# Spare accumulation banks behind each group of eight columns, mixer steps on ScalarE, and the output transfers in another order

## The chip, the cores and the metric
The kernel runs on one core of a Trainium2 chip. The metric is the time of one execution on the device in microseconds (us). Three runs of the kernel before took 987.56 to 987.98 us, with a median of 987.88 us.

## The reference
Two blocks of a transformer follow each other on one sequence of 256 tokens with 1024 channels, all in float32.

```
x = x + rms_norm(hybrid_mixer(rms_norm(x)) @ w_out)          # block 1: RG-LRU, gated linear
h = rms_norm(x)                                              # attention (GLA), causal softmax attention
x = x + rms_norm((silu(h @ w_gate) * (h @ w_up)) @ w_down)   # FFN 0
for l in (0, 1):                                             # block 2, with shifts and scales from c
    h = modulate(x, sh1, sc1)
    y = short_conv_mixer(h) if l == 0 else forgetting_attention(h, k, v, log_fcum)
    x = layer_norm(alpha * x + g1 * y)
    h = modulate(x, sh2, sc2)
    x = layer_norm(alpha * x + g2 * swiglu(h))               # FFN 1 and FFN 2
```

The widths of the FFNs are 2816. The second attention has 16 heads of 64. The gated linear attention works with the logarithm of a forget gate, `log_sigmoid(...) / 16`, which is summed along chunks of 64 tokens and goes through exponentials. The shifts, scales and gates of block 2 are products of `silu(c)` with matrices of 112 x 128 rows.

## The kernel before
All activations lie transposed, 128 channels by 256 tokens to a tile, so that x is eight tiles. Weights are streamed in blocks of 128 x 128; there are 2336 of them. Eight blocks come with one transfer of 512 KB (`raw_load`, line 127), issued on SyncE's (SP's) queue, into one of four buffers. To reach float32 accuracy, each weight and each activation is held as a high and a low part. `weights` (line 130) splits eight blocks at a time: ScalarE (ACT) copies them into the high part `wh` (line 144), and VectorE (DVE) subtracts to get the low part `wl` (line 150). There are five buffers for each part. A block then costs three matmuls on TensorE (PE): high by high, low by high and high by low (`mm3`, lines 162 to 164).

The results go to eight accumulation banks (PSUM). Four belong to the pool `pacc` (tiles named acc), two to `plg` (named lg), and two to `pms` (named ms, for small things). `single` (line 168) computes one output column of 128 channels in one acc bank, `pair` (line 176) two columns in one acc bank. `kouter` (line 223) computes eight columns at once, with the loop over the eight input tiles outermost, so that it can begin before all tiles of the input are there; it takes all four acc banks. `lazy` (line 1041) begins six columns of an FFN or of the key projection before the normalisation of its input is known, four in acc and two in lg banks.

Each FFN (`ffn`, line 900) has 22 pairs of a gate column and an up column. FFN 0 begins with a group of eight columns in `kouter` and goes on with 18 pairs. FFN 1 and FFN 2 have six lazy columns, then a group of eight, then 15 pairs. After each pair `evac` (line 906) reads the bank: in FFN 0 DVE multiplies both columns by the row R (lines 909 and 911), ACT applies silu (line 522), DVE multiplies (line 914), ACT makes the high part (line 921) and DVE the low part `ml` (line 922). In FFN 1 and 2 the multiplications by R fall away and line 918 reads the bank. The down projection (22 blocks to a column) follows. The convolution stage (lines 1201 to 1223) has 24 columns: a group of eight, and then singles.

The matrices of the shifts and scales are handled by `gemv` (line 360): one transfer of 512 KB for 128 rows, on SP's queue, into one of three buffers gw (line 368), and one product on DVE with a sum along the row (line 371). 112 of them are spread over the work by `fill` (line 184): after each column `grate` of them come due (`GR`, line 30: 0.75 per column in FFN 0, 1.2 in its down projection, 0.375 in the convolution stage, 0.9 and 1.05 in FFN 1 and its down projection, 1.4 in the second attention, 0.25 in FFN 2; a column of a down projection counts 2.75). In the second attention only the query columns from number 3 on count, five of them.

The order on every engine is written by a scheduler that simulates the program at compile time with modelled durations; it puts what is ready in the simulation first, and by the order of the program among what is ready. `after` (line 383) ties one instruction behind another on the same engine. Two sets of ties matter here. `unbroken` (line 377) sets `bound`, a list of instructions behind which the coming splits `wl` are put (after `free` of them), and `gbound`, the instruction behind which the coming products of `gemv` are put. In FFN 0 `gbound` is the end of the reciprocal root before it.

The second attention (lines 1304 to 1322) is written with a fixed order on PE. In step i of its loop PE computes the query column of pair i + 1, the logits of pair i, the transposes of the softmax of pair i - 1 (`fox_pt`, line 800), four blocks of the output projection, and the product with the values. The softmax (`fox_softmax`, line 784) takes four maxima on DVE (line 793), four exponentials on ACT (line 794), one reciprocal and four normalisations on DVE (line 797). Before the loop, splits are tied behind the forget gates; behind step 0, splits and products are tied behind the last maximum of pair 0.

In the mixer, `lru` (line 529) takes four taps of a convolution on DVE, `gla_decay` (line 599) adds a bias and divides by 16 on DVE (lines 607 and 615), and `gla` (line 618) masks the keys for four heads on DVE (line 643). At the end six output tiles are finished on DVE (lines 1355 and 1357) and tiles 0 and 1 on GpSimd (POOL) and ACT; each tile's transfer is issued on SP's queue (line 1358).

## Time and profile before

| what | value |
|---|---|
| median of three runs | 987.88 us |
| the profiled execution, its own time | 985.9 us |
| its span, from the first to the last instruction | 984.2 us |
| mean granted clock of PE | 0.979 of full speed |
| bytes moved by transfers | 219.56 MB, 223 GB/s over the span |

The profiled execution is one run of the program. Its time is the span and 1.7 us around it. A row of the timeline has the start and the length in us from the span's start, the engine, the line of the kernel, the operation with its output and inputs, and the count; in brackets stands how long the engine was idle before it and what ended that. Consecutive instructions of the same kind are merged into one row. The busy time of PE counts matmuls that overlap, so a busy PE is not PE at its peak.

### The profile page before, as it was taken

What the parts mean: (1) busy time and instruction counts of PE and PEld (TensorE: products, weight loads), DVE (VectorE), ACT (ScalarE), POOL (GpSimd) and SP (SyncE); (2) the same over time, 40 slices, a digit from 0 to 9 for tenths busy, and PEclk for the clock granted to TensorE, in tenths of its full rate; (3) what the DMA queues carried; (4) which work ended last, traced back from release to release, by engine and by line L of the source; (5) the groups of instructions that cost most, each with busy time, mean ns of one, the idle gap of its engine ahead of it and who ended that gap; (6) DMA issues with size and microseconds to landing.
All of it is one profiled execution on the core that took longest, in us unless ns stands there. A gap on an engine that the chain in (4) does not pass through costs nothing.

```text
span 984.2 us, 19003 instructions
## 1 busy us (share of the span) xinstructions
PE 927.9 (94%) x7434; PEld 893.6 (91%) x7434; DVE 768.8 (78%) x1471; ACT 530.2 (54%) x951; POOL 19.7 (2%) x66
## 2 busy tenths in 40 slices
PE   7989997999999999998899999999699999999996
PEld 7879896999999899998899999987587899999995
DVE  7896678999988588679899899796764897665553
ACT  7484653554444555548555454377365586554331
POOL 1111000000000000000000000000000000000001
PEclk9999998999999999999999999999799999999998
DMA  8754337899999477544999999454642257655531
GB/s 291 249 197 129 108 108 278 294 330 327 318 336 390 142 255 250 179 134 155 320 341 356 329 368 348 167 176 145 250 150 65 87 153 275 214 184 183 191 108 43
DMA packets 62346, 219.56 MB, mean 223 GB/s; under 512 B 7112, under 2 KB 8784, under 8 KB 62256
## 3 DMA queue, kind: packets, MB, share of 16 engines
q1 hardware_dynamic: 61056, 215.06, 63.7%
q0 software_dynamic: 1056, 3.16, 1.0%
q8 instruction: 58, 0.95, 0.4%
q14 instruction: 32, 0.26, 0.1%
q10 hardware_dynamic: 144, 0.13, 0.0%
HBM read 217.26 MB, written 2.63 MB: 223 GB/s over the span
## 4 chain that ended last, share of the span: by engine, by line
PE 80%; DVE 12%; ACT 4%; issue 3%; DMA 2%; DVEq 0%; ACTq 0%
PE acc L162 20%; PE acc L164 20%; PE acc L163 20%; PE acc L197 4%; DVE wl L150 4%; PE acc L198 4%; PE acc L203 3%; DMA raw<-wts 1%; ACT wh L144 1%; DVE gw L371 1%; PE acc L251 1%; PE acc L253 1%; PE acc L252 1%; PE ms L820 1%; PE lg L773 1%
## 5 line engine op out<-in xcount | busy, mean ns | idle before, releaser
L150 DVE TENSOR_TENSOR wl<-raw,wh 128x1024 fp32r<-128x1024 f32 (+2 forms) x296 | 356.2, 1209 | 102.4 <-ACT wh L144 101.0
L144 ACT ACTIVATE wh<-raw 128x1024 fp32r<-128x1024 f32 (+2 forms) x296 | 307.6, 1046 | 225.4 <-PE acc L164 128.2
L162 PE MATMUL acc<-yh,wh 128*128 128x256 f32 x608 | 171.1, 282 | 7.0 <-DVE ff_m L918 5.6
L162 PE MATMUL acc<-xh,wh 128*128 128x256 f32 x576 | 164.2, 285 | 8.9 <-DVE ff_u L911 7.2
L164 PE MATMUL acc<-yl,wh 128*128 128x256 f32 x608 | 171.3, 282 | 0.0
L163 PE MATMUL acc<-yh,wl 128*128 128x256 f32 x608 | 170.6, 281 | 0.0
L163 PE MATMUL acc<-xh,wl 128*128 128x256 f32 x576 | 162.9, 283 | 1.4 <-DVE wl L150 1.4
L164 PE MATMUL acc<-xl,wh 128*128 128x256 f32 x576 | 163.0, 283 | 0.0
L163 PE MATMUL acc<-mh,wl 128*128 128x256 f32 x528 | 148.1, 281 | 0.0
L164 PE MATMUL acc<-ml,wh 128*128 128x256 f32 x528 | 148.1, 281 | 0.0
L162 PE MATMUL acc<-mh,wh 128*128 128x256 f32 x528 | 147.9, 281 | 0.0
L371 DVE SCALAR_TENSOR_TENSOR gw<-gw,cact 128x1024 f32<-128x1024 f32 x112 | 134.7, 1221 | 0.6 <-DMA gw<-ada 0.4
L162 PEld LDWEIGHTS acc<-yh,wh 128*128 128x128 f32 x608 | 115.2, 190 | 7.6 <-DVE ff_m L918 6.1
L162 PEld LDWEIGHTS acc<-xh,wh 128*128 128x128 f32 x576 | 109.9, 191 | 11.3 <-DVE ff_u L911 7.4
L163 PEld LDWEIGHTS acc<-yh,wl 128*128 128x128 f32 x608 | 115.2, 190 | 0.4 <-issue 0.4
L164 PEld LDWEIGHTS acc<-yl,wh 128*128 128x128 f32 x608 | 114.9, 189 | 0.6 <-issue 0.6
L163 PEld LDWEIGHTS acc<-xh,wl 128*128 128x128 f32 x576 | 110.1, 191 | 1.8 <-DVE wl L150 1.6
L164 PEld LDWEIGHTS acc<-xl,wh 128*128 128x128 f32 x576 | 109.8, 191 | 0.1
L162 PEld LDWEIGHTS acc<-mh,wh 128*128 128x128 f32 x528 | 99.5, 189 | 0.0
L164 PEld LDWEIGHTS acc<-ml,wh 128*128 128x128 f32 x528 | 99.4, 189 | 0.0
L163 PEld LDWEIGHTS acc<-mh,wl 128*128 128x128 f32 x528 | 99.3, 188 | 0.0
L197 PE MATMUL acc<-xh,wh 128*128 128x256 f32 (+1 forms) x256 | 67.7, 294 | 8.7 <-ACT wh L144 5.5
(399 smaller groups left out, 1493.2 us busy)
## 6 DMA issues: line engine op xcount, KB each, us to landing
raw<-wts SPq DMA_DIRECT2D x288, 512.0 KB, 4.5
gw<-ada SPq DMA_DIRECT2D x112, 512.0 KB, 5.6
raw<-wts SPq DMA_DIRECT2D x6, 256.0 KB, 5.9
m_scr<-m_row POOLq DMA_DIRECT2D x2, 768.0 KB, 5.8
ax<-xT SPq DMA_DIRECT2D x4, 256.0 KB, 4.8
m_b<-m_scr POOLq DMA_DIRECT2D x8, 128.0 KB, 3.6
out<-fg SPq DMA_DIRECT2D x8, 128.0 KB, 1.8
cst<-cst SPq DMA_DIRECT2D x1, 588.5 KB, 7.1
```

Of the source, the lines that this page charges most:

```text
L144: i = self.aw = nc.scalar.activation(self.wh[:, d], r, AF.Copy)
L150: self.anchor = nc.vector.tensor_tensor(self.wl[:, d], r, self.wh[:, d].bitcast(F32), ALU.subtract)
L162: m = [mm(ps, wh, xh, start=start, stop=False), mm(ps, wl, xh, start=False, stop=False), mm(ps, wh, xl, start=False, stop=stop)]
L163: mm(ps, wl, xh, start=False, stop=False),
L164: mm(ps, wh, xl, start=False, stop=stop)]
L197: m.append(mm(outs[i], wh, X[0][k], start=k == 0 and i % per == 0, stop=False))
L198: m.append(mm(outs[i], wl, X[0][k], start=False, stop=False))
L203: m.append(mm(outs[i], wh, X[1][k], start=False, stop=False))
L251: mm(outs[tt], h, wh, start=k == 0 and (tt == 0 or not one), stop=False)
L252: mm(outs[tt], l, wh, start=False, stop=False)
L253: mm(outs[tt], h, wl, start=False, stop=k == NK - 1 and (tt == 1 or not one))
L371: i = nc.vector.scalar_tensor_tensor(t, t, 1.0, self.cact, op0=ALU.mult, op1=ALU.mult, accum_out=self.ada[:, g:g + 1])
```

## The change
`single` and `pair` get a switch that puts their result into an lg bank. The two pairs behind each group of eight in an FFN, and the two singles behind it in the convolution stage, use it. In `ffn`, `gbound` becomes the last write of each evacuation. In the second attention, splits are tied behind the last normalisation of an earlier pair and products behind that of the pair just issued. In the mixer the first tap of the convolution (two instructions), the bias of the gate (one) and the head masks (four) go from DVE to ACT, and the division by 16 goes into the scale of the exponentials. The output transfers are issued behind the loop in a given order.

```diff
+OUT = (2, 3, 4, 5, 0, 6, 1, 7)
...
-    def single(self, wname, c, X, nk=NK, fill=True):
-        t = self.acc([P, T])
+    def single(self, wname, c, X, nk=NK, fill=True, spare=False):
+        t = self.tl(self.plg, [P, T], "lg") if spare else self.acc([P, T])
...
-    def pair(self, w0, c0, w1, c1, X):
-        t = self.acc([P, 2, T])
+    def pair(self, w0, c0, w1, c1, X, spare=False):
+        t = self.tl(self.plg, [P, 2, T], "lg") if spare else self.acc([P, 2, T])
...
-            V.tensor_scalar(xc, xpad[:, 0:T], self.vec("lru_conv_w", t), self.vec("lru_conv_b", t), ALU.mult, ALU.add)
+            A.activation(xc, xpad[:, 0:T], AF.Identity, scale=self.vec("lru_conv_w", t), bias=self.vec("lru_conv_b", t))
...
-        V.tensor_scalar(z[:, 0:T], zp, self.vec("gla_gate_b", 0), None, ALU.add)
+        self.nc.scalar.activation(z[:, 0:T], zp, AF.Identity, bias=self.vec("gla_gate_b", 0))
...
-        la = la[:, 0:T]
-        V.tensor_scalar(la, la, 1.0 / 16.0, None, ALU.mult)
-        return la
+        return la[:, 0:T]
...
-        A.activation(ex, cum, AF.Exp)
+        A.activation(ex, cum, AF.Exp, scale=1.0 / 16)
...
-        A.activation(en, cum, AF.Exp, scale=-1.0)
+        A.activation(en, cum, AF.Exp, scale=-1.0 / 16)
...
-            V.tensor_scalar(kd[:, h, :], en, self.hmask[:, h:h + 1], None, ALU.mult)
+            A.activation(kd[:, h, :], en, AF.Copy, scale=self.hmask[:, h:h + 1])
...
-        A.activation(kx, df, AF.Exp)
+        A.activation(kx, df, AF.Exp, scale=1.0 / 16)
...
-        A.activation(dec, c3[:, :, 63], AF.Exp)
+        A.activation(dec, c3[:, :, 63], AF.Exp, scale=1.0 / 16)
...
-            V.tensor_scalar(Ls[hh][:, s], Ls[hh][:, s], sm[:, 2 * hh + j:2 * hh + j + 1], None, ALU.mult)
+            self.alast = V.tensor_scalar(Ls[hh][:, s], Ls[hh][:, s], sm[:, 2 * hh + j:2 * hh + j + 1], None, ALU.mult)
...
-            V.tensor_tensor(lo, m, h.bitcast(F32), ALU.subtract)
+            self.gbound = V.tensor_tensor(lo, m, h.bitcast(F32), ALU.subtract)
...
-            ps = self.pair(wg, j, wu, j, X)
+            ps = self.pair(wg, j, wu, j, X, j < n + 6)
...
-                    got[(w, i)] = self.single(w, i, X)
+                    got[(w, i)] = self.single(w, i, X, spare=(w, i) in order[8:10])
...
-        self.unbroken([self.gbound], 2)
+        al = self.gbound
+        self.unbroken([al], 2)
...
-                if i == 0:
-                    self.unbroken([self.gbound, self.mxs], 0)
+                if i < NK:
+                    self.bound, self.gbound, al = [al], self.alast, self.alast
...
-            nc.sync.dma_start(self.a["out"][k], z)
         self.pipeline(seq)
+        for k in OUT:
+            nc.sync.dma_start(self.a["out"][k], zs[k])
```

## Rows read from the trace of the kernel before

**Rows 1.** The page's first part: span, busy time and share of each engine.

```profile
span 984.2 us, 19003 instructions
...
PE 927.9 (94%) x7434; PEld 893.6 (91%) x7434; DVE 768.8 (78%) x1471; ACT 530.2 (54%) x951; POOL 19.7 (2%) x66
```

**Rows 2.** Waits of PE: line, what it waited for, us in total, times, longest.

```profile
PE ms L805 <- DVE a_L L797: 9.8, 2, 9.5
PE acc L162 <- DVE ff_u L911: 7.2, 1, 7.2
PE acc L162 <- DVE ff_m L918: 5.6, 2, 3.7
```

**Rows 3.** Timeline of PE, the matmuls behind its long stalls.

```profile
164.46 0.58 PE L162 MATMUL acc<-xh,wh 128*128 128x256 f32 x1 [7.24 <-DVE ff_u L911]
...
360.76 0.39 PE L162 MATMUL acc<-xh,wh 128*128 128x256 f32 x1 [1.10 <-DVE c_up L1215]
...
478.47 0.39 PE L162 MATMUL acc<-yh,wh 128*128 128x256 f32 x1 [3.68 <-DVE ff_m L918]
...
701.83 0.48 PE L805 MATMUL ms<-ident,a_L 128*128 128x128 f32 x1 [9.50 <-DVE a_L L797]
...
821.65 0.38 PE L162 MATMUL acc<-yh,wh 128*128 128x256 f32 x1 [1.97 <-DVE ff_m L918]
```

**Rows 4.** Stretches behind stalls: length, PE busy, granted clock, DMA share, GB/s.

```profile
164.46:168.89 4.43, 4.43 (x21) 0.50 1.02 409
...
478.47:482.50 4.03, 4.03 (x22) 0.63 1.00 407
...
701.83:706.50 4.67, 4.33 (x18) 0.50 0.93 374
...
70.00:74.00 4.00, 3.53 (x12) 0.59 0.36 94
```

**Rows 5.** Timeline of DVE in FFN 0, behind the group of eight.

```profile
157.94 1.22 DVE L371 SCALAR_TENSOR_TENSOR gw<-gw,cact 128x1024 f32<-128x1024 f32 x1
...
163.65 0.43 DVE L909 TENSOR_TENSOR ff_g<-acc,R 128x256 f32<-128x256 f32 x1
```

**Rows 6.** FFN 0 behind the group: busy time of PE, PEld, DVE, ACT and POOL.

```profile
155.67:267.50 111.83, 104.59 (x874) 104.40 (x873) 106.62 (x184) 53.02 (x79) 0.00 (x0) 0.97 0.89 310
```

**Rows 7.** Timeline of DVE in FFN 1, behind the group of eight.

```profile
474.58 2.36 DVE L150 TENSOR_TENSOR wl<-raw,wh 128x1024 fp32r<-128x1024 f32 x2
...
476.85 1.22 DVE L371 SCALAR_TENSOR_TENSOR gw<-gw,cact 128x1024 f32<-128x1024 f32 x1
```

**Rows 8.** Timeline of DVE in FFN 2, behind the group of eight.

```profile
818.73 2.55 DVE L150 TENSOR_TENSOR wl<-raw,wh 128x1024 fp32r<-128x1024 f32 x2 [0.81 <-ACT wh L144]
```

**Rows 9.** Timeline of DVE in the second attention, softmax of pair 0.

```profile
687.38 0.75 DVE L793 TENSOR_REDUCE a_mx<-lg 128x1 f32<-128x256 f32 x2
...
695.93 0.18 DVE L795 RECIPROCAL a_sm<-a_sm 128x4 f32<-128x4 f32 x1
...
701.22 1.01 DVE L797 TENSOR_SCALAR a_L<-a_L,a_sm 128x256 f32<-128x256 f32 x4
```

**Rows 10.** Pairs 2 to 6 of that attention: busy times as in rows 6.

```profile
709.75:748.00 38.25, 38.25 (x332) 33.77 (x331) 25.29 (x69) 25.79 (x78) 0.00 (x0) 1.00 0.38 125
```

**Rows 11.** Mixer: a stall of PE, and instructions that move or are like them.

```profile
69.97 1.23 PE L730 MATMUL lg<-a_k,a_q 64*128 64x256 f32 x4 [2.40 <-DVE a_k L1136]
...
66.82 1.14 DVE L643 TENSOR_SCALAR g_kd<-g_en,hmask 128x256 f32<-128x256 f32 x4
...
L607 DVE TENSOR_SCALAR g_z<-ms,vec 128x256 f32<-128x256 f32 x1 | 0.5, 466 | 0.0
...
L1217 ACT ACTIVATE c_y<-c_up,vec 128x256 f32<-128x256 f32 x8 | 3.9, 499 | 0.0
```

**Rows 12.** Timeline at the end: last tiles on DVE, last output transfer.

```profile
979.65 0.87 DVE L1357 SCALAR_TENSOR_TENSOR fg<-fg,vec,ln_w 128x256 f32<-128x256 f32 x2
...
981.08 0.40 SPq L1358 DMA_DIRECT2D out<-fg  x1
```

**Rows 13.** Waits of SP's queue from 670 to 750 us.

```profile
SPq L368 <- DVE gw L371: 12.8, 6, 8.5
```

## The prediction, made before the change was built

> **What bounds the kernel now.** I began with the busy times. TensorE (PE) is busy for 94% of the span and VectorE (DVE) for 78% [rows 1], so what can be won cheaply is the time in which PE stands still or runs slowly. The waits of PE name that time: one wait for a_L of line 797, one for ff_u of line 911 and two for ff_m of line 918 make 22.6 us together [rows 2]. The timeline of PE says where they are: a stall of 7.24 us after the first group of eight columns in FFN 0, 3.68 us at the same place in FFN 1, 1.97 us in FFN 2, 1.10 us in the convolution stage and 9.50 us at the first head pair of the second attention [rows 3]. In the first four, PE wants an accumulation bank that the evacuation has not yet read; in the last it wants the normalised softmax of pair 0.
>
> A stall costs more than itself, which the granted clock shows [rows 4]. Behind the 7.24 us stall PE ran 4.43 us at 0.50 of full speed (1.2 of 2.4 GHz), behind the 3.68 us stall 4.03 us at 0.63, behind the 9.50 us stall 4.67 us at 0.50. As time times what is missing from 1, that is 2.2, 1.5 and 2.3 us. Behind 1.97 us of standing still no such stretch is to be seen: I add nothing there.
>
> **The spare banks and the evacuations first.** In FFN 0 the first evacuation starts at 163.65 us, and ahead of it in DVE's order stand four splits of weights (line 150) and four products for the modulation vectors (line 371), the first at 157.94 [rows 5]. PE's last matmul of the group was over near 157.2 (164.46 less 7.24). With two spare banks the next two pairs need no evacuation; with the new order (gbound moved to each evacuation's last write) the products go behind the evacuations. So the bank wait goes, for 7.2 + 2.2 = 9.4 us. What is late next is the split weights. In the 111.8 us from there to the end of FFN 0, DVE is busy for 106.6 [rows 6], so it has 5.2 us to spare, and 9.4 us less time leaves it 4.2 us short. If the products slip into the down projection behind it nothing is given back, if they stay all 4.2 us are. I can't tell which, and take the middle: a gain of 7.3 us, ends 5.2 and 9.4.
>
> In FFN 1 the same sum is 3.7 + 1.5 = 5.2 us. There two splits start at 474.58 us, just when PE becomes free (478.47 less 3.68 is 474.79), and a product stands between them and the evacuation [rows 7]. The first split is done 1.2 us later, so if the products are moved behind and nothing else is, PE still waits about 0.9 us: a gain of 4.3 us, ends 2.3 (both splits waited for, and some of the slow stretch kept) and 5.2. In FFN 2 two splits end at 821.28 us, 0.4 us ahead of PE's start, and the first of them near 820.0 [rows 8]; whichever the spare pair needs, the gain lies between 0.4 and 2.0 us. I take 1.5, since the first is nearer to the order in which pairs consume groups. In the convolution stage two single columns go to the spare banks: 1.0 us of the 1.10, ends 0 and 1.1. These four make 7.3 + 4.3 + 1.5 + 1.0 = 14.1 us.
>
> **The second attention.** PE comes to the transposes of pair 0 at 692.33 us (701.83 less 9.50) [rows 3]. DVE takes the first maximum at 687.38, but the reciprocal runs only at 695.93 and the four normalisations at 701.22, for 1.01 us [rows 9]; between maximum and reciprocal the timeline has three products and three splits of 1.22 us. After the change no product that is issued in the loop may run before the normalisation of the pair before it, and splits only behind that of two pairs back. From pair 2 on 7 products (five columns at 1.4 each) fall behind normalisations, instead of filling the gap in pair 0. Without those six (7.3 of 8.55 us) the reciprocal comes between 688.6 and 690 (the exponentials on ACT have to end too), and the normalisations are over by 691, before PE asks. So the stall of 9.5 us and the slow 2.3 us go: 11.8 us. Added are ordering waits: behind each normalisation stand up to two products and one or two splits, at 1.22 us each. Their cover is DVE's idle time: from 709.75 to 748 it is busy 25.3 of 38.25 us [rows 10], 13 us free against 7 x 1.22 = 8.5 us of products. They fit, but a maximum that waits for a product delays PE directly, so I keep back 2.3 us for this and for weights that are now split later: a gain of 9.5, ends 4 and 11.8.
>
> **The four mixer steps.** What leaves DVE: four head masks (1.14 us in a row, 0.29 each), one bias (0.47), two first taps of the convolution and one scaling, which I price like a mask: 1.14 + 0.47 + 3 x 0.29 = 2.5 us [rows 11]. The scaling by 1/16 costs nothing in its new place: it is a constant of exponentials that run anyway. Onto ScalarE (ACT) come seven instructions: by the nearest row, a copy with a column as scale at 0.50 us, 3.5 us in all. What is gained is what PE waits for: a stall of 2.40 us for a_k at 69.97, with the four masks a little ahead of a_k on DVE, and 4 us at a clock of 0.59 behind it (1.6 us) [rows 4, 11]. Bounds: 4.0 us if stall and slow stretch go, minus 1.0 us if the seven stand on the path at 3.5 us where 2.5 stood. I take 1.0, near the 1.14 us by which a_k comes sooner. The trace has an ACT step of this kind at 0.50 us against 0.29 us for a mask on DVE. The Trainium skill (ScalarE: Activation LUTs, Rules for kernel authors) says to multiply and add on VectorE and not on ScalarE; the trace agrees for the instruction alone, and by that rule this term would be the minus 1.0 us, and the sum 2.0 us less.
>
> **The output order.** The last tile is ready at about 980.52 us and its transfer is issued at 981.08; the issues before it follow one another without a pause of the queue [rows 12]. A better order has at most 0.5 us to give; a tile put ahead of one that was ready sooner costs as much. I take 0.
>
> **Sum.** 14.1 + 9.5 + 1.0 + 0 = 24.6 us. The profiled execution took 985.9 us (span 984.2 and 1.7 around it), 2.0 us less than the median of 987.9: it comes to 961.3, and by the median to 963.3 us, which is my number.
>
> **Rivals.** *Splits take the place of banks* (0.17). For: DVE has only 5.2 us free in FFN 0 [rows 6], and in FFN 1 the splits come just in time [rows 7]. Against: the products are no one's input until a later stage and can slip. Then the FFN terms of 13.1 us shrink to about 4: 972.4 us.
> *The new order makes PE wait in every head pair* (0.12). For: products and splits crowd behind each normalisation. Against: DVE's 13 free us [rows 10]. One us in each of seven pairs leaves 2.5 of the 9.5 us: 970.3 us.
> *ScalarE becomes the late engine of the mixer* (0.08). For: each step is longer there [rows 11]. If what DVE saves is hidden and the 3.5 us stand whole on the path, the term goes from plus 1.0 to minus 3.5: 967.8 us. The skill's rule above points this way.
> *Slower: transfers pile up in SP's queue* (0.04). The loads of weights and of modulation rows share one queue in order; before, a modulation load once held it for 8.5 us until a product freed its buffer [rows 13]. Products that are pinned behind evacuations free their buffers later, and weights behind them arrive later, in each of the 33 pairs of FFN 0 and FFN 1. From 0.75 us per pair (24.6 over 33) on, the gain is eaten; at 1.0 us the time is 963.3 + 33 = 996 us. Against: five buffers of split weights stand ahead of PE, and none of its long waits is for a split [rows 2].
> *The change doesn't take effect* (0.03): the planner of the order keeps the evacuations late, or the spare banks are themselves in use, and the time stays within 2 us of 987.9.
>
> **Numbers.** The forecast has 0.56, the rivals 0.17, 0.12, 0.08, 0.04 and 0.03. With the best ends of all terms (9.4 + 5.2 + 2.0 + 1.1 + 11.8 + 4.0 + 0.5 = 34.0) the time is 953.9, with the worst (5.2 + 2.3 + 0.4 + 0 + 4 - 1.0 - 0.5 = 10.4) it is 977.5. All ends on one side are unlikely, so the range is 955 to 976, which takes in the first three rivals. A difference of 0.2% is about what a measurement of this kernel can tell from none. Faster by more: 0.93; within: 0.03; slower: 0.04.
>
> **What would show it.** Right: in the profile after, no wait of PE for ff_u, ff_m or a_L above 1 us, no stretch at half clock behind the groups of eight, products in the second attention spread over pairs 2 to 6, DVE above 96% busy in FFN 0. Wrong: waits of PE for wl of line 150 in FFN 0 and FFN 1, waits for a_L in every pair, or idle time of ACT's or DVE's splits that ends with a load of raw weights.

## The result, and the profile after

The changed kernel took 952.85 us (median of three runs, 952.66 to 953.45) against 987.88 us: a ratio of 0.9647 with a 95% interval of 0.9626 to 0.9669, 35.0 us less. The forecast was 963.3 us, with a range from 955: the sign and the places were right, the gain was 10.4 us larger than forecast, and the time lies 2.15 us below the range. The profiled execution took 952.66 us with a span of 950.8. Spans are compared below; theirs differ by 33.4 us, and the other 1.6 us is mostly that the profiled execution of before was 2.0 us under its median.

The page of the changed kernel (its first part), then its waits of PE:

```profile
span 950.8 us, 18969 instructions
...
PE 916.2 (96%) x7434; PEld 884.6 (93%) x7434; DVE 765.5 (81%) x1463; ACT 529.7 (56%) x958; POOL 19.9 (2%) x66
```

```profile
PE acc L198 <- ACT wh L145: 5.5, 1, 5.5
PE ms L309 <- DVE nw_y L290: 2.4, 3, 1.3
PE acc L198 <- DVE fg L971: 2.2, 1, 2.2
PE acc L199 <- DVE wl L151: 2.0, 3, 0.9
PE acc L198 <- ACT xh L267: 1.8, 1, 1.8
```

Line numbers up to some 600 are one higher than before, later ones mostly one lower. No wait for ff_u, ff_m, c_up or a_L is left of those that stood at the head [rows 2, 3]; the 5.5 us for wh is the program's start. DVE does nearly the same work (765.5 against 768.8 us) in a shorter span [rows 1].

The timeline of PE gives the length of each stage. The marks are the same instructions in both traces: the broadcast behind a norm's reciprocal root (L308, L309 after), the last statistic of a down projection (L299, L300), the first matmul of a group (in FFN 2 the one behind its first wait), the first matmul of wv with a low part of weights (the expectations call it the first block of wv), and in the lazy columns of FFN 2 the matmul behind their wait for fg (there called the first lazy column).

| stretch on PE | before | after | gain |
|---|---|---|---|
| start to the broadcast at the end of the mixer | 131.1 | 128.1 | 3.0 |
| to the last statistic of FFN 0's down projection | 200.6 | 191.2 | 9.4 |
| to the first group of the convolution stage | 4.9 | 7.1 | -2.2 |
| to the first group of FFN 1, behind its lazy columns | 112.5 | 110.5 | 2.0 |
| to wv | 203.3 | 198.2 | 5.1 |
| second attention and wo, to the lazy columns behind | 122.5 | 109.9 | 12.6 |
| these lazy columns, to the group of FFN 2 | 23.0 | 21.8 | 1.2 |
| FFN 2, to its last statistic | 172.8 | 170.5 | 2.2 |
| to the end of the span | 13.6 | 13.6 | 0.0 |

FFN 0 after, in two stretches (length, busy PE, PEld, DVE, ACT, POOL, clock, DMA share, GB/s):

```profile
157.24:165.00 7.76, 7.76 (x68) 7.76 (x67) 6.85 (x14) 5.88 (x10) 0.00 (x0) 1.00 0.84 295
165.00:215.00 50.00, 50.00 (x428) 50.00 (x427) 50.00 (x90) 25.28 (x37) 0.00 (x0) 1.00 0.90 317
...
215.00:264.00 49.00, 49.00 (x420) 49.00 (x419) 45.85 (x78) 23.56 (x35) 0.00 (x0) 1.00 0.93 324
```

PE never stands still behind the group and its clock stays at 1.0, although DVE is busy for the whole of the first 50 us. That is the surprise of the result: [rows 6] had made me fear that a full DVE would hold PE up. What gave way were the products of `gemv`. Between the end of the mixer and the first matmul of the down projection DVE did 30 of them before and 24 after (busy time and mean in ns behind the bar):

```profile
L371 DVE SCALAR_TENSOR_TENSOR gw<-gw,cact 128x1024 f32<-128x1024 f32 x30 | 35.8, 1220 | 0.0
```

```profile
L372 DVE SCALAR_TENSOR_TENSOR gw<-gw,cact 128x1024 f32<-128x1024 f32 x24 | 28.8, 1220 | 0.0
```

Six products, 7.0 us of DVE's time, slipped into the down projection: three stand within it (19 products instead of 16) and three behind its last statistic.

The softmax of pair 0, on DVE, after:

```profile
668.25 0.87 DVE L792 TENSOR_REDUCE a_mx<-lg 128x1 f32<-128x256 f32 x2 [1.64 <-PE lg L780]
...
670.57 0.18 DVE L794 RECIPROCAL a_sm<-a_sm 128x4 f32<-128x4 f32 x1 [0.53 <-ACT a_L L793]
670.79 1.01 DVE L796 TENSOR_SCALAR a_L<-a_L,a_sm 128x256 f32<-128x256 f32 x4
```

From the first maximum to the normalisation it is 2.5 us instead of 13.8 [rows 9]. One thing became worse, the end of FFN 0's down projection, where three products of `gemv` now stand between the steps of the reciprocal root and of the normalisation (DVE after, then PE after, then the same two matmuls of PE before):

```profile
320.63 0.16 DVE L290 SCALAR_TENSOR_TENSOR nw_y<-nw_q,nw_y 128x2 f32<-128x2 f32 x1
...
320.96 1.22 DVE L372 SCALAR_TENSOR_TENSOR gw<-gw,cact 128x1024 f32<-128x1024 f32 x1
...
323.72 1.22 DVE L372 SCALAR_TENSOR_TENSOR gw<-gw,cact 128x1024 f32<-128x1024 f32 x1
```

```profile
322.66 0.68 PE L309 MATMUL ms<-ident,nw_y 128*128 128x128 f32 x4 [1.31 <-DVE nw_y L290]
...
326.42 0.39 PE L198 MATMUL acc<-xh,wh 128*128 128x256 f32 x1 [1.77 <-ACT xh L267]
```

```profile
333.90 0.68 PE L308 MATMUL ms<-ident,nw_y 128*128 128x128 f32 x4 [0.17 <-DVE nw_y L289]
...
336.64 0.39 PE L197 MATMUL acc<-xh,wh 128*128 128x256 f32 x1 [0.75 <-ACT xh L266]
```

### The profile page after: what moved, and what is told of

It reads as the page before. It is cut to its first block, busy times and chain, and to the rows that moved or that the text cites. A ratio compares the mean times of both kernels' runs of the same rounds, so it can differ in the third digit from the quotient of the medians.

```text
span 950.8 us, 18969 instructions
## 1 busy us (share of the span) xinstructions
PE 916.2 (96%) x7434; PEld 884.6 (93%) x7434; DVE 765.5 (81%) x1463; ACT 529.7 (56%) x958; POOL 19.9 (2%) x66
## 4 chain that ended last, share of the span: by engine, by line
PE 84%; DVE 8%; ACT 3%; issue 2%; DMA 2%; SPq 0%; DVEq 0%; ACTq 0%
PE acc L165 19%; PE acc L163 19%; PE acc L164 19%; PE acc L198 4%; PE acc L199 4%; PE acc L204 4%; DVE wl L151 3%; PE lg L165 1%; PE lg L163 1%; PE lg L164 1%; DMA raw<-wts 1%; PE acc L254 1%; PE acc L252 1%; PE acc L253 1%; ACT wh L145 1%
## 5 line engine op out<-in xcount | busy, mean ns | idle before, releaser
L163 PE MATMUL acc<-yh,wh 128*128 128x256 f32 x544 | 152.3, 280 | 0.9 <-ACT yh L267 0.9
L165 PE MATMUL acc<-yl,wh 128*128 128x256 f32 x544 | 152.6, 281 | 0.5 <-DVE yl L268 0.5
L164 PE MATMUL acc<-yh,wl 128*128 128x256 f32 x544 | 151.9, 280 | 0.0
L163 PE MATMUL acc<-xh,wh 128*128 128x256 f32 x528 | 148.7, 282 | 0.0
L165 PE MATMUL acc<-xl,wh 128*128 128x256 f32 x528 | 148.3, 281 | 0.0
L164 PE MATMUL acc<-xh,wl 128*128 128x256 f32 x528 | 148.0, 280 | 0.0
L163 PEld LDWEIGHTS acc<-yh,wh 128*128 128x128 f32 x544 | 102.4, 188 | 1.1 <-ACT yh L267 1.1
L165 PEld LDWEIGHTS acc<-yl,wh 128*128 128x128 f32 x544 | 102.1, 188 | 0.8 <-DVE yl L268 0.7
L164 PEld LDWEIGHTS acc<-yh,wl 128*128 128x128 f32 x544 | 102.5, 188 | 0.0
L164 PEld LDWEIGHTS acc<-xh,wl 128*128 128x128 f32 x528 | 99.5, 189 | 0.3
```

The source lines that it names most:

```text
L163: m = [mm(ps, wh, xh, start=start, stop=False), mm(ps, wl, xh, start=False, stop=False), mm(ps, wh, xl, start=False, stop=stop)]
L164: mm(ps, wl, xh, start=False, stop=False),
L165: mm(ps, wh, xl, start=False, stop=stop)]
```

## Experiments

Each run was compared with the kernel before on the same chip (medians of 985.9 to 987.8 us there). "Alone" is an edit to the kernel before; the others are edits to the changed kernel, where nothing else is said. Intervals are of 95%.

### One part undone

The second attention with its old ties:

```diff
-        al = self.gbound
-        self.unbroken([al], 2)
+        self.unbroken([self.gbound], 2)
...
-                if i < NK:
-                    self.bound, self.gbound, al = [al], self.alast, self.alast
+                if i == 0:
+                    self.unbroken([self.gbound, self.mxs], 0)
```

> The changed kernel with the old ties of the second attention (splits and products behind the last maximum of pair 0). Theory A (all stalls and the slow stretches behind them are gone and nothing came back): the 9.5 us stall returns with its slow stretches, 12 to 13 us slower than the changed kernel, 965 to 966 us. Theory B (the attention is worth the 9.5 us of the prediction, and the rest of the surplus came from elsewhere): 962 to 963 us.

Measured: 962.42 us, ratio 0.976 (0.9734 to 0.9787), some 11 us above the changed kernel by the ratios. The stall is back at 9.38 us for a_L. The ties are what removes it. The time lies where theory B put it. In the profile the attention is 8.7 us longer than in the changed kernel (118.6 against 109.9), and the convolution stage, which had not been edited, 1.5 us longer, with PE at half clock for 3.4 us in it.

The spare banks off, the tie of the products kept:

```diff
-            ps = self.pair(wg, j, wu, j, X, j < n + 6)
+            ps = self.pair(wg, j, wu, j, X)
...
-                    got[(w, i)] = self.single(w, i, X, spare=(w, i) in order[8:10])
+                    got[(w, i)] = self.single(w, i, X)
```

> The changed kernel without spare banks, products still tied behind the evacuations. Theory A (the order alone brings the evacuation forward, the banks carry the rest): PE waits 3 to 4 us in FFN 0, 1 to 2 us in FFN 1, under 1 us in FFN 2, 1 us in the convolution stage, 6 to 9 us slower in all with the slow stretches, 959 to 962 us. Theory B (the banks carry all of it): the full 7.2, 3.7, 2.0 and 1.1 us return with 3.7 us of slow stretches, about 970 us. Theory C (the order carries all): 953 to 954 us.

The spare banks kept, the tie off:

```diff
-            self.gbound = V.tensor_tensor(lo, m, h.bitcast(F32), ALU.subtract)
+            V.tensor_tensor(lo, m, h.bitcast(F32), ALU.subtract)
```

> The changed kernel with spare banks, but without the tie of products behind evacuations in the FFNs. Theory A (the banks give PE two pairs, 11 us, of work, and the evacuations behind four products come in time): within 3 us of the changed kernel, 953 to 956 us. Theory B (products ahead of evacuations still stop PE behind the two pairs): 4 to 8 us slower, 957 to 961 us.

Measured: 962.01 us (ratio 0.9752, 0.9732 to 0.9772) without the banks, 969.25 us (0.9825, 0.9809 to 0.9841) without the tie: some 10 and 18 us above the changed kernel by the ratios. Timelines of PE, first without banks, then without the tie:

```profile
159.23 0.58 PE L163 MATMUL acc<-xh,wh 128*128 128x256 f32 x1 [3.79 <-DVE ff_u L910]
```

```profile
194.97 0.55 PE L163 MATMUL acc<-xh,wh 128*128 128x256 f32 x1 [6.27 <-DVE ff_u L910]
```

With the tie alone half of the 7.24 us [rows 3] is left, as theory A of the first run said. The second run is slower than either of its theories allowed. With the banks alone the stall only moves, from the first pair to later ones. DVE's groups between 150.9 and 195 us say why (busy time and mean in ns behind the bar), without the tie and then in the changed kernel:

```profile
L372 DVE SCALAR_TENSOR_TENSOR gw<-gw,cact 128x1024 f32<-128x1024 f32 x12 | 14.3, 1213 | 0.0
```

```profile
L372 DVE SCALAR_TENSOR_TENSOR gw<-gw,cact 128x1024 f32<-128x1024 f32 x7 | 8.4, 1220 | 0.0
```

Five more products, 5.9 us, stand ahead of the evacuations, about the length of the stall. FFN 0 with its down projection is 8.8 us longer than in the changed kernel. Two banks put the wait off; the order removes it. The second attention was 10 us longer there too, though nothing in it had been edited; that is taken up below.

The four mixer steps as before:

```diff
-            A.activation(kd[:, h, :], en, AF.Copy, scale=self.hmask[:, h:h + 1])
+            V.tensor_scalar(kd[:, h, :], en, self.hmask[:, h:h + 1], None, ALU.mult)
...
```

> The changed kernel with the four mixer steps as before. Theory A (the mixer was worth the 3.0 us by which PE reaches the end of that stage sooner): 955.5 to 956.5 us. Theory B (that time is the scheduler's new order and not the steps): 952.5 to 954 us, or a time that lies far off both.

Measured: 955.91 us (0.9687, 0.9667 to 0.9708), 4 us above the changed kernel by the ratios, while in the profiles the mixer ended 7.05 us later, at 135.19 us, and so 4.1 us later than with these steps in the kernel before. PE ran at half clock for 10.2 us in this mixer and for 3.4 us in that of before. One profile of the mixer is not to be trusted to 2 us.

The output transfers in their loop again:

```diff
+            nc.sync.dma_start(self.a["out"][k], z)
         self.pipeline(seq)
-        for k in OUT:
-            nc.sync.dma_start(self.a["out"][k], zs[k])
```

> The changed kernel with the output transfers issued as before, each in the loop in the order of the tiles. My prediction's step (the queue hands the transfers out one behind the other in either order, and the last tile sets the end): the stretch from the last statistic of the last down projection to the end of the span is as long as in the changed kernel, 13.5 us, within 0.3 us; time within 0.5 us of the changed kernel. Rival (the order matters): 0.5 us or more longer at the end.

Measured: 952.29 us (0.9647, 0.962 to 0.9674). From the last statistic to the end it is 13.6 us, as with the new order and as before. The new order is worth nothing that can be seen.

### The mixer

All four steps of the change alone, and then only the line that is turned back above, the head masks, alone:

> The kernel before with the four mixer steps alone on ScalarE or in the scales. Theory A (the steps themselves are worth what the mixer gained in the changed kernel): 3.0 us less, ratio 0.997; the 2.40 us wait for a_k falls below 1 us and PE's clock behind it stays above 0.9. My prediction's step: 1.0 us less, ratio 0.999, with the wait for a_k shorter by about 1.1 us. Rival (the mixer's gain is an accident of the order that the scheduler found in the changed kernel, where the same steps put back cost 7 us): anything between 2 us more and 5 us less, with another order on PE in the mixer and the wait for a_k still above 2 us.

> The kernel before with the four head masks alone on ScalarE. Theory M (the masks stand ahead of a_k in DVE's order, and PE's 2.40 us wait for a_k is what the mixer's change takes away; behind that wait the clock was 0.50 to 0.59 for 4 to 10 us in the profiles of the old steps): wait for a_k down to about 1.2 us or less, no stretch under 0.75 behind it, mixer (start of the second norm broadcast to its end) at 96 to 98 us against 99 to 103 in the profiles of the old steps; 2 to 5 us less than before, ratio 0.995 to 0.998. Rival (the other three steps, the first taps and the scaling, open the way): wait for a_k above 2 us, ratio 1.000.

Measured: all four steps alone 981.33 us (0.995, 0.9934 to 0.9966), 4.9 us less; the masks alone 984.86 us (0.9974, 0.9953 to 0.9995), 1.9 us less. The wait for a_k is 2.40 us before, 0.56 with all steps and 1.59 with the masks alone. Windows around this wait (the one from 70 to 74 us in the kernel before is in [rows 4]), for the kernel before, the kernel with the ties of the second attention alone (whose mixer is that of before) and the changed kernel:

```profile
74.00:80.00 6.00, 5.67 (x47) 5.57 (x48) 5.96 (x28) 3.42 (x12) 2.20 (x4) 1.00 0.44 138
```

```profile
66.00:70.00 4.00, 1.61 (x14) 1.38 (x14) 3.97 (x16) 3.21 (x6) 2.34 (x6) 0.92 0.59 200
70.00:74.00 4.00, 3.38 (x12) 2.09 (x11) 3.99 (x13) 1.88 (x9) 0.06 (x1) 0.50 0.44 99
74.00:80.00 6.00, 5.92 (x27) 5.64 (x28) 5.96 (x26) 2.79 (x11) 2.20 (x4) 0.54 0.41 127
```

```profile
70.00:74.00 4.00, 2.91 (x21) 2.20 (x22) 4.00 (x14) 3.41 (x11) 0.06 (x1) 1.00 0.49 116
74.00:80.00 6.00, 6.00 (x51) 5.66 (x49) 5.76 (x24) 3.56 (x11) 2.25 (x4) 1.00 0.40 114
```

Behind the old stall PE ran at or near half clock (1.2 GHz) for 4 us in the profile of before and for 10 us in the second, with the same instructions; in the kernel with 22 idle matmuls below, whose mixer is the same too, there was no slow stretch behind the same wait of 2.40 us. From the first norm's broadcast to the last, the mixer took 99.0 to 101.6 us, mean 100.2, in six profiles with the old steps in the kernel before, and 95.9 to 97.6, mean 96.5, in twelve with the new ones. So the steps are worth 3.7 us, and the profile of before had caught one of the short slow stretches. With the old steps six of seven profiles (these six and that of the changed kernel with the old steps) have a slow stretch there, of 3.4 to 10.2 us; with the new ones three of twelve have one, of 3.4 us each. With the masks alone the wait is only a third shorter, yet in their one profile the mixer took 96.8 us without a slow stretch; by the times they bring 1.9 of the 4.9 us. One profile can't show whether the masks end the slow stretch. Which of the other three steps shortens the wait further was not tried.

### The slow stretch by itself

Idle matmuls in the stall of FFN 0, in the kernel before, 22 and then 30:

```diff
+        if l == 0:
+            wt, wp = self.tl(self.plg, [P, T], "lg"), self.lastm
+            for _ in range(22):
+                wi = nc.tensor.matmul(wt[:, 0:P], self.ident, self.ident, start=True, stop=True)
+                self.after(wi, wp)
+                wp = wi
         for j in range(n + 4, NFF):
```

> The kernel before with 22 matmuls of the identity by itself into an unused lg bank, behind the group of eight of FFN 0, so that PE works through most of the 7.24 us in which it stood still there; no bank comes free sooner and no result is used. Theory A (the slow 4.43 us behind the stall are a second price of the stall, worth 2.2 us): the clock behind the group stays at 1.0, the first pair starts at the same time as before or up to 1 us later, and FFN 0 ends 1.2 to 2.2 us sooner; time 1 to 2 us less, ratio 0.998 to 0.999. Rival (the slow stretch has another cause, or DVE and not PE sets the pace behind the group): the stretch stays at 0.50, or it goes and FFN 0 ends at the same time; ratio 1.000.

> As the kernel with 22 idle matmuls in the stall of FFN 0, with 30 of them, so that less than 0.7 us of the 7.24 us stall is left (2.32 us were left with 22, and the clock behind was still down to 0.62 for 4.5 us). Theory A (the slow stretch is the price of PE standing still, and nothing else): clock 1.0 behind the group, the first pair starts within 0.5 us of where it did, and the span from the start of FFN 0's group to the end of its down projection is 1.8 to 2.3 us shorter than before (200.6 us before), time about 2 us less. Rival (the slow stretch costs little, since behind the stall DVE is late anyway): the clock is up and the stage is at most 0.8 us shorter than before.

Measured: 985.26 us (0.9992, 0.9977 to 1.0008) and 985.38 us (0.9985, 0.9968 to 1.0001). Neither shows a difference by its times, so the stage has to speak: FFN 0 with its down projection takes 200.6 us before, 200.2 with 22 matmuls, 198.7 with 30. The waits left were 2.32 and 0.53 us. The window behind the wait, with 22 and with 30:

```profile
164.00:168.50 4.50, 4.07 (x21) 4.07 (x22) 4.50 (x13) 2.31 (x6) 0.00 (x0) 0.62 1.03 419
```

```profile
167.81:172.31 4.50, 4.50 (x38) 4.50 (x39) 4.50 (x12) 2.87 (x7) 0.00 (x0) 1.00 1.02 411
```

No bank came free sooner: the first pair started 33.3 us behind the end of the mixer, with 30 matmuls as before. And yet 1.9 us were won once PE kept working, while five profiles with this stage as before lie between 200.6 and 201.3 us. The slow stretch is a price of its own, 2.2 us by [rows 4].

### The second attention, and the FFNs, alone

The part of the change's diff in the second attention alone, and then its parts in `single`, `pair`, `ffn` and the convolution stage alone:

> The kernel before with one edit: the ties of the second attention (splits behind the normalisation of an earlier pair, products behind that of the pair just issued). Everything else as before. Theory A (the 9.50 us stall and its slow stretch of 2.3 us go whole, and the 1.37 us wait of PE for wl behind the logits goes with them; nothing is given back because the moved products fit in DVE's idle time): 11.8 to 13.2 us less than before, ratio 0.987 to 0.988, no wait of PE for a_L above 1 us. My prediction's step (2.3 us given back): 9.5 us less, ratio 0.990. Rival (the ties only work together with the tie of the products in the FFNs, since without that one the attention was 10 us longer): at most 4 us less, ratio above 0.996, with waits for wl or a_pt of 1 to 2 us each.

> The kernel before with the spare banks and the products tied behind the evacuations alone (FFNs and convolution stage); mixer, second attention and outputs as before. Theory A (the stages add up as in the changed kernel: 9.4 in FFN 0, minus 2.2 at the end of its down projection, 2.0 in the convolution stage, 5.1 in FFN 1, 2.2 in FFN 2): 16.5 us less than before, ratio 0.983, and the 9.5 us stall of the second attention stays. My prediction's terms: 14.1 us less, ratio 0.986. Rival (part of the second attention's gain comes from the products that the FFN tie moves, not from its own ties): 19 us or more, ratio below 0.981, with a stall for a_L well under 9 us.

Measured: the ties of the attention alone 982.09 us (0.9959, 0.9941 to 0.9976), only 4.1 us less. The banks and ties of the FFNs alone 966.64 us (0.9802, 0.9787 to 0.9818), 19.5 us less, and their stall for a_L is still there with 10.19 us. The length of the attention scatters with its slow stretches: it was 118.6 to 122.5 us, mean 120.7, in seven profiles with the old ties, and 107.7 to 109.9, mean 108.7, in eleven with the new ones in which the loads below were early. With the FFNs alone it was 119.1. In the first of the two runs the normalisation of pair 0 ran at 692.42, 8.8 us sooner than in [rows 9], and PE's wait for it was gone. In its place stood a wait of 2.50 us for a_pt, and one of 1.53 us for wl (1.37 before). SP's queue, its longest wait and a wait of ACT with the attention's ties alone:

```profile
687.72 1.47 SPq L368 DMA_DIRECT2D gw<-ada  x2
690.04 6.05 SPq L127 DMA_DIRECT2D raw<-wts  x3
```

```profile
SPq L368 <- DVE gw L371: 9.5, 2, 8.7
```

```profile
695.03 1.06 ACT L144 ACTIVATE wh<-raw 128x1024 fp32r<-128x1024 f32 x1 [2.85 <-DMA raw<-wts]
```

The same queue in the changed kernel, whose logits of pair 0 start at 666.74 us (686.47 above):

```profile
664.35 1.47 SPq L369 DMA_DIRECT2D gw<-ada  x2
666.67 7.80 SPq L128 DMA_DIRECT2D raw<-wts  x3
```

Two loads of modulation rows wait until two products free their buffers. The products are tied behind the forget gates, whose logarithm ACT takes 6.6 us ahead of the logits in the changed kernel but 3.0 us ahead in the other. (In eleven of twelve profiles with the products tied in the FFNs it is 6.4 to 9.9 us, in one 3.8; in all eight without that tie 2.3 to 3.2.) Three loads of weights wait behind those two loads, ACT's copies wait for the weights, and exponentials stand behind the copies on ACT. This is the rival of SP's queue that I had priced for the slower side [rows 13], in one place and at 6.7 us: the attention took 116.6 us against 109.9. The kernel without the tie in the FFNs has the same picture (loads of gw at 674.69, 1.2 us behind its logits). To test it, the two products were untied from the gates, still without the parts in the FFNs (shown against the kernel with the attention's ties alone):

```diff
-            self.gbound = self.fox_gates(fz)
+            gates = self.fox_gates(fz)
...
-        al = self.gbound
+        al = gates
         self.unbroken([al], 2)
```

> As the kernel with the ties of the second attention alone, and besides the two products that stood behind the forget gates are no longer tied there. Theory Q (in the kernel with the ties alone the two products came late, at 686.46 us behind the gates, so the two loads of modulation rows on SP's queue went out at 687.72 and the three loads of weights behind them only from 690.04; ACT's copies of those weights, which stand ahead of exponentials, waited 2.85 and 0.77 us, and PE with them): the products run over 5 us sooner, the loads of weights go out before the logits of pair 0 start, no wait of ACT for a raw load above 1.5 us, and the attention (from the first block of wv to the first lazy column behind it) is 109 to 111 us long as in the changed kernel, against 116.6; time 11 to 13 us less than before, ratio 0.987 to 0.989. Rival (ACT's order in the loop is at fault, not the queue): within 2 us of the kernel with the ties alone, ratio 0.994 to 0.998.

Measured: 971.49 us (0.9841, 0.9813 to 0.9869), 14.5 us under before. That is 10.4 us more than with the tie, 12.1 by the spans of the two profiles. Of these 8.6 are in the attention (116.6 to 107.9 us), 2.0 in the mixer and 1.2 in the lazy columns; the last two are scatter. The queue:

```profile
665.82 1.47 SPq L368 DMA_DIRECT2D gw<-ada  x2
672.78 19.51 SPq L127 DMA_DIRECT2D raw<-wts  x6
```

ACT's longest wait for a weight in the first two pairs is 1.49 us. So theory Q holds, and the queue cost more than I had expected.

### Slack, and versions that go further

Six runs on the changed kernel: more products due in the pairs of FFN 0 and as many fewer in its down projection (the first diff), fewer columns with products in its down projection (the second), none of either, the gates untied as above, this and the second diff together, and the first diff again.

```diff
-GR = (0.75, 1.2, 0.375, 0.9, 1.05, 1.4, 0.25)
+GR = (1.0, 0.655, 0.375, 0.9, 1.05, 1.4, 0.25)
```

```diff
-            ps = pre[c] if c < len(pre) else self.single(wname, c, X, nk, c < (6 if nk > NK else 5))
+            ps = pre[c] if c < len(pre) else self.single(wname, c, X, nk, c < 5)
```

> The changed kernel with 36 instead of 27 products due in the pairs of FFN 0 and as many fewer in its down projection: 9 x 1.22 = 11 us more work for DVE, in a stage in which it was already busy all the time. Theory A (products stand behind evacuations and splits and are nobody's input there, so they slip on and on; DVE has slack whatever its busy time says): FFN 0 and its down projection stay within 0.7 us of the 191.2 us of the changed kernel, no wait of PE above 1 us in them, the products run on into the down projection; time within 1 us of the changed kernel. My prediction's step (what DVE is short of delays PE): PE waits for wl in FFN 0, at least 4.2 us and up to 11 us more; ratio 0.969 to 0.976.

> The changed kernel with products of modulation vectors issued behind five instead of six columns of FFN 0's down projection, so that three or so fewer stand at its end. Theory A (the 2.16 us that the changed kernel loses between the last statistic of that down projection and the first group of the convolution stage come from three products that DVE has in its order between the steps of the reciprocal root and of the normalisation): the stretch from the statistic to the group falls from 7.08 to 4.9 us, time 2.1 us under the changed kernel, ratio to before 0.9625. Rival (the products are only moved and stop PE elsewhere): the stretch shortens and another grows by as much, time within 0.5 us of the changed kernel.

> The changed kernel itself, on the same chip and in the same rounds as the one with fewer products: a control. 0.9647 of before, within its interval of 0.9626 to 0.9669; stages within 0.2 us of those of its first profile, except the mixer, whose length differed by up to 1.2 us between profiles of the same instructions.

> The changed kernel, the two products of the second attention no longer tied behind the forget gates. Theory Q (that tie costs wherever the gates are late; in the changed kernel they come 3.5 us sooner than in the kernel before, so less is left to win): the attention, 109.9 us from the first block of wv to the first lazy column behind it, falls to 107.9 us as it did with the ties of the attention alone, time 2 us under the changed kernel, ratio 0.9625. Rival (in the changed kernel the loads are early enough already: the loads of weights go out 0.07 us before the logits of pair 0): no difference above 0.5 us.

> The changed kernel with both edits: the two products not tied behind the gates, and fewer products at the end of FFN 0's down projection (1.1 us of the 2.2 us there were left at the attention). If both add up: 2.0 + 1.1 = 3.1 us under the changed kernel, ratio 0.9615. Rival (the products left out there come due elsewhere and stop the attention again): no better than the better of the two.

> The kernel with 36 products in the pairs of FFN 0 a second time, beside the kernel that differs from the changed one in its outputs alone. If the 2.2 us at the end of FFN 0's down projection are really won (its first run had 950.16 us, and the stretch from the statistic to the first group of the convolution stage was 4.91 instead of 7.08 us): 1 to 2 us under the other kernel of this call. Rival (chance of one run): within 0.5 us of it.

| kernel | us | ratio | interval |
|---|---|---|---|
| changed kernel again | 951.80 | 0.9646 | 0.9619 to 0.9673 |
| fewer products in FFN 0's down projection | 951.60 | 0.9640 | 0.9613 to 0.9667 |
| the two products free of the gates | 952.78 | 0.9659 | 0.9639 to 0.9678 |
| both of these | 950.94 | 0.9637 | 0.9617 to 0.9658 |
| more products in FFN 0 | 950.16 | 0.9631 | 0.9613 to 0.9650 |
| more products in FFN 0, second run | 950.01 | 0.9622 | 0.9600 to 0.9645 |

With nine more products due in the pairs of FFN 0, DVE did three more there (27 instead of 24), 3.9 us, and let the rest slip; the down projection had 19 in both kernels. FFN 0 with its down projection took 191.7 instead of 191.2 us, PE's longest wait in it was 0.47 us:

```profile
215.00:264.00 49.00, 49.00 (x419) 49.00 (x418) 48.41 (x82) 22.65 (x32) 0.00 (x0) 1.00 0.98 354
```

So three more products cost PE 0.5 us in a stage in which DVE had had 3.2 us to spare from 215 to 264 us and now had 0.6. The others cost nothing because they slipped; what DVE could have taken on if they had stayed, the run doesn't show. And since no product was left for the end of the down projection, that end was clear: 4.9 instead of 7.1 us to the next group. Fewer products there by themselves cleared it as well, but a third of the 2.2 us came back as a wait of 0.54 us and other small ones in the convolution stage, and the times of the two kernels don't differ (951.60 and 951.80 us). Both edits together are no better than this one alone. Untying the gates gained nothing in the changed kernel (109.6 us of attention against 109.9, and 108.5 in its second run), as its rival said: the loads are early enough there. The version with more products in FFN 0 is the fastest of the study, 2.3 us under the kernel beside which it ran the second time, which differs from the changed one in its outputs alone; the intervals of the two overlap, so I call it likely and not shown.

## Why the prediction fell short

**Right.** The places: all stalls of [rows 3] went, and so did the slow stretches behind them. The idle matmuls show for FFN 0 that these are paid on top of the wait. No rival with splits in place of banks or waits in every pair appeared, and the output order is 0.

**The step that failed** is one that I made four times: taking something off because DVE looked full. "If the products slip into the down projection behind it nothing is given back, if they stay all 4.2 us are. I can't tell which, and take the middle": in the FFN itself nothing was given back. The gain was 9.4 us, the upper end. Of my two outcomes the first came: six products, 7.0 us, slipped, and DVE's busy time was no limit, because nobody waits for products in this stage. It was partly paid where I had not looked: 2.2 us at the end of the down projection, where three of the six came to stand, as the run with fewer products there shows. FFN 0 net of that is 7.2 us, my 7.3 by accident. In FFN 1 (5.1 against 4.3) the 0.9 us kept for a split was not needed, and in FFN 2 (2.2 against 1.5) neither was the half us kept for one. The convolution stage (2.0 against 1.0) is another matter: a second wait of 0.38 us went too, which I had not counted, and where the rest came from is open, since its clock was 1.0 before and after. One count was wrong, without weight in the sum: ahead of the first evacuation the trace of before has three products and not four.

**The second attention** gained 12.6 us in the two profiles, 12.0 in the means of many, and not 9.5. "I keep back 2.3 us" was again for DVE; the moved products fitted, as [rows 10] had let me compute. The slow stretch was priced too low as well. My window in [rows 4] ends at 706.50 us, but PE was at half clock until 708.18:

```profile
701.83:708.18 6.35, 6.01 (x26) 4.88 (x27) 2.90 (x14) 1.95 (x7) 0.00 (x0) 0.50 0.68 275
```

That is 3.2 us and not 2.3, and 9.5 + 3.2 makes 12.7. A wait of PE for wl of 1.37 us ahead of the stall, which I had left out, went too; waits for a_pt of 1.01 and 0.64 us came. But the attention's ties alone gave 4.1 us. That the whole gain came is due to a neighbour that I had not linked to it: with the products tied in the FFNs the compile-time order takes the forget gates sooner, and with them the loads on SP's queue. Why it does so was not looked into. My sum of parts hid this, since the parts alone make 4.1 + 4.9 + 19.5 = 28.5 us and together 35.0.

**The mixer.** "I take 1.0, near the 1.14 us by which a_k comes sooner" was too small: 3.0 us in the two profiles, 3.7 in the mean of many. The wait fell by 1.84 us and slow stretches became rarer. The Trainium skill (ScalarE: Activation LUTs, Rules for kernel authors) would have multiplications on VectorE. By the instruction it is right here too, a mask took 0.51 us on ACT against 0.36 on DVE (0.43 against 0.29 as a share of the four in a row [rows 11]; the prediction set one instruction of ACT against a share of DVE's row). But PE's wait for a_k hung on DVE, and with the steps on ACT the stage gained.

**The lazy columns** behind the attention gave 1.2 us that no step foresaw. They are no gain of the change: the kernel with 30 idle matmuls, which has the order of before there, took 21.8 us for them as well, and a version of the changed kernel 23.0. It is the clock (0.93 or 1.00) from one run to the next.

**The range.** The best ends summed to 953.9 us and I dropped them because "all ends on one side are unlikely". They weren't independent. One assumption, that a full DVE delays PE, stood behind four subtractions (2.1 in FFN 0, 0.9 in FFN 1, 0.5 in FFN 2, 2.3 in the attention), and it fell for all at once. These make 5.8 us, less the 2.2 us at the end of the down projection; the spans gained 8.8 us more than my 24.6. The rest are terms that I had too small or at nothing: the mixer by 2.0, the lazy columns by 1.2, the convolution stage by 1.0, the attention's slow stretch by 0.9. So even the best ends would have missed the time, by 1.0 us.

The Trainium skill (Perfetto Trace Analysis, Matmul Optimizations) advises to use all eight PSUM banks. The runs agree that the banks are needed (some 10 us without them), and add that they are not enough: without the order of the evacuations the stall only moved.

## What to carry to other kernels

A busy share says that an engine works, not that anybody waits for it: split it into work with a consumer in this stage and work that may slip, and take off only the first. When several terms of a sum rest on one assumption, give the range its two joint outcomes instead of treating the ends as independent. After moving work, look at the end of the stage into which it slips, and at in-order queues of transfers whose buffers it frees.

## What the runs showed of the hardware

A wait of 2.32 us was followed by 4.5 us at a clock of 0.62, one of 0.53 us by none (both with idle matmuls ahead), while behind 1.97 us in FFN 2 [rows 3] the clock was 1.00 for 4.35 us:

```profile
821.65:826.00 4.35, 4.34 (x36) 4.35 (x37) 3.39 (x8) 3.13 (x8) 0.00 (x0) 1.00 0.99 380
```

The length of the wait alone doesn't decide: in the second attention of the changed kernel a wait of 0.94 us for yh was followed, 2 us later, by 3.4 us at half clock, and with the old mixer steps in that kernel a wait of 0.95 us at the same place by none. Matmuls whose result nobody uses, into an unused bank, kept the clock at 1.0 behind the group of FFN 0. With the same instructions the stretch behind one stall of 2.40 us lasted 4 us in one profile and 10 in another, and in a third there was none, so a stall of this size has a price that one profile can misstate by some 2 us.
